# Seven-product down projection for 6 of 22 K pairs, its weight sums in the room of the transposed input, and operand tiles at one 2 KB remainder

## The chip, the cores and the metric

The kernel runs on one core of one Trainium2 chip. The metric is the device time of one execution in microseconds (us); of several executions the median is taken. The engines of the core are TensorE (PE; its loads of the stationary operand are PEld), VectorE (DVE), ScalarE (ACT), GpSimd (POOL) and SyncE (SP), whose queue issues nearly all transfers.

## What is computed

Two layers of a residual trunk over 256 tokens of width 2048. All data are float32.

```python
def swiglu(h, w_gate, w_up, w_down):
    return (jax.nn.silu(h @ w_gate) * (h @ w_up)) @ w_down

for l in range(DEPTH):                                   # 2 layers
    h = rms_norm(x, pre_mix_norm[l])
    m = hybrid_mixer(h, l, w_in[l], w_o[l], ...)          # stick-breaking and differential attention
    x = x + rms_norm(m, post_mix_norm[l])
    h = rms_norm(x, pre_ffn_norm[l])
    f = swiglu(h, w_gate[l], w_up[l], w_down[l])          # 2048 -> 5632 -> 2048
    x = x + rms_norm(f, post_ffn_norm[l])
```

The change concerns `@ w_down`: a product of 256 tokens x 5632 with 5632 x 2048, once in each layer.

## The kernel before

**Weights.** Every weight matrix is streamed once, in pieces of 256 rows (a K pair: two K blocks of 128) by 512 columns, 512 KB each. A piece lands in one of four `raw` buffers. A float32 piece is split in two: ACT rounds it to `hi` (L171), DVE forms the rest `lo = raw - hi` (L173). Both are of the type float32r. The stationary operands are split in the same way (`jh` and `jl` for the down projection, L852 and L854), and one float32 block product is three matmuls on PE, hi with hi, hi with lo, lo with hi, each of a 128x128 stationary and a 128x512 moving operand. `feed` prepares pieces four ahead of the one in use (`LOOKAHEAD`), six `hi` and six `lo` buffers hold them.

**Gate and up.** Eleven chunks `c` of 512 columns; in each, eight K pairs `kp`. For a K pair there are two token tiles, two K blocks and two matrices, hence eight block products, 24 matmuls (`eight`). For K pairs 2, 4 and 6 (in chunk 0: 4 and 6) a form with seven products is used (`seven`, 21 matmuls). It needs four sums of weights, formed on DVE (`mixed_weights`: `T`, L145) and split into `Th` (ACT, L154) and `Tl` (DVE, L156); four sums of token blocks (`token_sums`: `f` L738, `s` L741 to L744), split into `sh` (ACT, L746) and `sl` (DVE, L748); and four more PSUM banks, whose contents are combined on DVE at the end of a chunk (L811 to L815). `T`, `Th` and `Tl` (8, 12 and 12 KB of each partition) lie in the pool `gu`, which lives only through gate and up. In chunk 0 the two K pairs 0 and 1, then the `token_sums` of K pairs 2, 4 and 6 together, stand ahead of the other K pairs.

**Down.** Two halves, each of two column chunks of 512 (`cc`), over 22 K pairs (`nkp`). For each K pair `down` issues 24 matmuls (L872, L873, L875) into four PSUM banks. `prep` makes `jh` and `jl` up to two K pairs ahead. In the second half the last three K pairs (`TAIL`) are worked off one bank after the other (L894 to L896), so that a bank's result can be finished (`evac_chunk`: square with sum on ACT, L343; times the gain on DVE, L347) while PE works on the next. `rescale` then forms the norm and adds to `x`; in layer 0 the new `x` is transposed for the next layer (L274, L277, L282), in layer 1 it is stored (L363).

**Transposed input.** `xT` is 16 tiles of 2 KB of each partition, in the pool `wpool`, which lives through the whole kernel. It holds the input of the mixer, then that of gate and up; during down its room is reserved for the next layer's input, which is written at the end of down.

**Order.** The instructions of an engine run in the order in which the built program has them. A scheduler sets that order from the order in the code and its own estimates; `high_priority` and `manual_schedule` pin some of it. `tick` counts steps of the main matmul loop, and side work (attention, the transposes `flip` of each activated chunk) is started so many ticks later.

Of the kernel before, what the change touches and what calls it, by code (L numbers as in the profile page):

```python
# [37 lines left out]
FIRST_ORDER = (0, 1, 3, 2, 4, 5, 6, 7)  # L38

WARM = 13  # L40

# [6 lines left out]
def kernel(  # L48
# [152 lines left out]
    idle = const.tile([P, CW], BF16, name="idle")  # L201
# [10 lines left out]
    lams = const.tile([P, 4, L * 64], F32, name="lams")  # L212
    negones = const.tile([P, P], F32, name="negones")
# [6 lines left out]
    def late_constants():  # L220
# [16 lines left out]
        lprod = const.tile([P, 2, L * 64], F32, name="lprod")  # L237
        lsum = const.tile([P, 2, L], F32, name="lsum")
# [13 lines left out]

    eps = const.tile([P, 1], F32, name="eps")
# [38 lines left out]
    def x_tiles(nm):  # L292
        return [wpool.tile([P, 2, S], F32R, tag="xT", bufs=KT, name=f"{nm}_{k}") for k in range(KT)]
# [47 lines left out]
    def evac_chunk(pool, acc, mg, ssm, gpost, c, t, nm, mpool=None):  # L341
        junk = pool.tile([P, CW], F32, tag="t2", name=f"jm_{nm}_{t}_{c}")
        nc.scalar.activation(junk, acc, AF.Square, accum_out=ssm[t][:, c : c + 1])  # L343
        if c % 2 == 0:
            mg[t, c // 2] = (mpool or pool).tile([P, 2, CW], F32, tag="qk", bufs=4, name=f"mg_{nm}_{t}_{c}")
# [249 lines left out]
    def settle(pool, rs, evac):  # L595

        for t, h in ((0, 0), (0, 1), (1, 0), (1, 1)):
            load_x(t, h)
            yield 1
        late_constants()  # L600
        rs += [inv_rms(t, pool, "in0") for t in range(NT)]
        yield 2
        scales(rs)
        evac()
# [73 lines left out]

    xT = None
    for l in range(L):  # L680
# [52 lines left out]
        def token_sums(kp):  # L733

            f = pool.tile([P, 2, S], F32, tag="t2", name=f"f{l}_{kp}")
            for kk in range(2):
                st = xT[2 * kp + kk]
                nc.vector.tensor_tensor(out=f[:, kk, :], in0=st[:, 0, :].bitcast(F32), in1=st[:, 1, :].bitcast(F32), op=ALU.add)  # L738
            a11, a21, a12, a22 = f[:, 0, 0:P], f[:, 0, P:S], f[:, 1, 0:P], f[:, 1, P:S]
            s = pool.tile([P, 4, P], F32, tag="t2", name=f"s{l}_{kp}")  # L740
            nc.vector.tensor_tensor(out=s[:, 0, :], in0=a21, in1=a22, op=ALU.subtract)  # L741
            nc.vector.tensor_tensor(out=s[:, 1, :], in0=s[:, 0, :], in1=a11, op=ALU.subtract)
            nc.vector.tensor_tensor(out=s[:, 2, :], in0=a11, in1=a21, op=ALU.subtract)
            nc.vector.tensor_tensor(out=s[:, 3, :], in0=s[:, 1, :], in1=a12, op=ALU.add)  # L744
            sh = gu.tile([P, 4, P], F32R, tag="sh", bufs=len(SEVEN), name=f"sh{l}_{kp}")
            nc.scalar.activation(sh, s, AF.Copy)  # L746
            sl = gu.tile([P, 4, P], F32R, tag="sl", bufs=len(SEVEN), name=f"sl{l}_{kp}")
            nc.vector.tensor_tensor(out=sl, in0=s, in1=sh.bitcast(F32), op=ALU.subtract)  # L748
            forms[kp] = (sh, sl)

        def product(a, stat, moving, first, last):
            sh, sl = stat
            hi, lo = moving
            nc.tensor.matmul(a, sh, hi, start=first, stop=False)  # L754
            nc.tensor.matmul(a, sh, lo, start=False, stop=False)  # L755
            nc.tensor.matmul(a, sl, hi, start=False, stop=last)  # L756
# [11 lines left out]
        def seven(banks, extra, c, kp, first, last):  # L768
            hi, lo = weights(plan[l]["gate"][c, kp], LOOKAHEAD)
            m = weights(plan[l]["up"][c, kp], LOOKAHEAD)  # L770
            e, o = xT[2 * kp], xT[2 * kp + 1]
            sh, sl = forms[kp]
            s1, s2, s3, s4 = ((sh[:, j, :], sl[:, j, :]) for j in range(4))
            p1, p6, p7, q5 = extra
            todo = (
                (p1, (e[:, 0, 0:P], e[:, 1, 0:P]), (hi[:, 0, :], lo[:, 0, :]), first, last),
                (banks[0], (o[:, 0, 0:P], o[:, 1, 0:P]), (hi[:, 1, :], lo[:, 1, :]), False, False),
                (q5, s1, m["t1"], first, last),
                (p7, s3, m["t3"], first, last),
                (p6, s2, m["t2"], first, last),  # L780
                (banks[1], s4, m["b22"], False, False),
                (banks[2], (o[:, 0, P:S], o[:, 1, P:S]), m["t4"], False, False),
            )
            for n, job in enumerate(todo):
                if n % 2 == 0:
                    tick()
                product(*job)

        for c in range(FF // CW):
# [3 lines left out]
            if c == 0:  # L793
                for t in range(NT):
                    for kp in order[:2]:
                        eight(banks, c, kp, (t,), kp == order[0], False)
                for kp in SEVEN:
                    token_sums(kp)
                order = order[2:]
            extra = None  # L800
            for kp in order:
                if kp not in mine:
                    eight(banks, c, kp, range(NT), kp == 0, kp == order[-1])
                    continue
                if kp == mine[0]:
                    extra = four_banks(1 - c % 2, [f"{q}_{l}_{c}" for q in ("p1", "p6", "p7", "q5")])
                seven(banks, extra, c, kp, kp == mine[0], kp == mine[-1])
                if kp == mine[-1]:
                    p1, p6, p7, q5 = extra
                    w = [pool.tile([P, CW], F32, tag="t2", name=f"w{j}_{l}_{c}") for j in range(4)]  # L810
                    nc.scalar.copy(w[0], p1)  # L811
                    nc.vector.tensor_tensor(out=w[1], in0=p6, in1=w[0], op=ALU.add)
                    nc.vector.tensor_tensor(out=w[2], in0=p7, in1=w[1], op=ALU.add)
                    nc.vector.tensor_tensor(out=w[1], in0=q5, in1=w[1], op=ALU.subtract)
                    nc.vector.tensor_tensor(out=w[3], in0=q5, in1=w[2], op=ALU.subtract)  # L815
# [18 lines left out]
        gu.release()  # L834
        dn = tc.alloc_tile_pool(name=f"dn{l}", bufs=4, reuse_waits="tile")
# [6 lines left out]
        xT = x_tiles(f"xI{l}") if l + 1 < L else None  # L842

        for half in range(2):
            split = {}

            def prep(kp):
# [7 lines left out]
                split[kp] = (jh, jl)  # L855

            cc = (2 * half, 2 * half + 1)
            got = four_banks(1 - half, [f"dn{l}_{c}_{t}" for c in cc for t in range(NT)])
            accs = {(c, t): got[2 * (c % 2) + t] for c in cc for t in range(NT)}

            def down(kp, toks):
# [4 lines left out]
                for kk in range(2):  # L866
                    tick()
# [8 lines left out]

            tail = TAIL if half == 1 else 0
            for kp in range(nkp - tail):
                down(kp, range(NT))
            for t in range(NT):  # L880
                if not tail:
                    for c in cc:
                        evac_chunk(pool, accs[c, t], mg, ssm, gpost, c, t, f"d{l}", dn)
                    continue
                for c in cc:
# [11 lines left out]
                    with tc.high_priority(offset=URGENT):  # L897
                        evac_chunk(pool, accs[c, t], mg, ssm, gpost, c, t, f"d{l}", dn)
                with tc.high_priority(offset=URGENT):
                    rescale(mg, ssm, t, f"d{l}", store if xT is None else lambda t, c: transposed(t, (l + 1) * KT, xT, cols=(c,)))  # L900
        if l + 1 < L:
            rs = [inv_rms(t, pool, f"in{l + 1}") for t in range(NT)]
        dn.release()
# [50 lines left out]
```

## Time and profile before

| | |
|---|---|
| median of 3 runs | 2244.42 us (2244.08 to 2244.92) |
| the profiled execution | 2242.9 us, its span 2241.2 us |
| granted TensorE clock over the span | 0.997 |
| PE busy | 2223.1 us, 99% |
| DVE busy | 1623.8 us, 72% |
| ACT busy | 1221.8 us, 55% |
| moved by DMA | 423.72 MB, mean 189 GB/s |

A group row names line, engine, operation, result<-operands, their shapes and the count; behind the bar stand busy time and the mean of one in ns, then the idle time ahead of them and what ended it. A windows row gives for a stretch of time its length, then for each engine its busy time and (x) how many instructions ran, the granted clock as a share of full speed, the DMA share and GB/s. A timeline row gives the start, the time, engine, line, operation and operands; in brackets the idle time before it and who ended it. Matmuls overlap: a matmul's shown time is from its start to the modelled end of its results, so the distance from start to start tells the rate. DVE's instructions overlap by a little as well.

### The profile page before, as it was taken

To read this page: it belongs to the slowest core of one execution; us is meant where nothing else is said; L and a number is where in the kernel's file an instruction comes from. 1 tells how busy PE (TensorE), PEld (TensorE's weight loads), DVE (VectorE), ACT (ScalarE), POOL (GpSimd) and SP (SyncE) were. 2 spreads that over 40 slices of the span, in tenths; PEclk is the share of its full clock that TensorE was granted. 3 is DMA by queue.
4 is the path that set the end of the run, shared out by engine and by line. 5 is a ranking of instruction groups with operands and counts; after the bars stand their busy time and mean duration, and the time that the engine had idled before them with its cause. 6 is when DMAs were issued, how large, how long until landed. Compare 5 with 4: busy or idle time off the path is not lost.

```text
span 2241.2 us, 27963 instructions
## 1 busy us (share of the span) xinstructions
PE 2223.1 (99%) x10189; PEld 1829.8 (82%) x10189; DVE 1623.8 (72%) x2209; ACT 1221.8 (55%) x1819; POOL 37.0 (2%) x76
## 2 busy tenths in 40 slices
PE   9999999999999999999999999999999999999998
PEld 7788888788888888888887888887888888888887
DVE  6666555899899898565576665559998998975555
ACT  6555554665555556444565455546654555554443
POOL 1100000000000000000010000000000000000000
PEclk9999999999999999999999999999999999999999
DMA  8655555466556556555565555554666556565553
GB/s 295 191 165 163 160 188 185 134 205 213 192 188 215 198 188 224 189 189 197 178 195 163 173 157 168 186 181 147 210 204 205 189 197 207 191 215 189 194 198 134
DMA packets 217996, 423.72 MB, mean 189 GB/s; under 512 B 13569, under 2 KB 14081, under 8 KB 217345
## 3 DMA queue, kind: packets, MB, share of 16 engines
q1 hardware_dynamic: 217712, 421.91, 56.6%
q8 instruction: 80, 1.31, 0.2%
q14 instruction: 60, 0.48, 0.1%
q10 hardware_dynamic: 144, 0.02, 0.0%
HBM read 419.77 MB, written 2.10 MB: 188 GB/s over the span
## 4 chain that ended last, share of the span: by engine, by line
PE 95%; ACT 2%; DVE 1%; DMA 1%; issue 0%; SPq 0%; DVEq 0%; ACTq 0%
PE c L755 10%; PE c L756 10%; PE c L754 10%; PE in L336 8%; PE in L338 8%; PE in L337 8%; PE dn L872 7%; PE dn L873 7%; PE dn L875 7%; PE o L338 2%; PE o L336 2%; PE o L337 2%; PE p L754 2%; PE p L755 2%; PE p L756 2%; PE actT_ps L829 1%
## 5 line engine op out<-in xcount | busy, mean ns | idle before, releaser
L173 DVE TENSOR_TENSOR lo<-raw,hi 128x1024 fp32r<-128x1024 f32 x719 | 872.3, 1227 | 328.2 <-ACT hi L171 322.5
L171 ACT ACTIVATE hi<-raw 128x1024 fp32r<-128x1024 f32 x719 | 748.7, 1056 | 473.2 <-PE c L756 167.2
L754 PE MATMUL c<-hi,xF 128*128 128x512 f32 x960 | 377.1, 393 | 0.3
L756 PE MATMUL c<-hi,xF 128*128 128x512 f32 x960 | 374.4, 391 | 0.0
L755 PE MATMUL c<-lo,xF 128*128 128x512 f32 x960 | 373.9, 390 | 0.0
L872 PE MATMUL dn<-hi,jh 128*128 128x512 f32 x656 | 255.6, 390 | 0.0
L873 PE MATMUL dn<-lo,jh 128*128 128x512 f32 x656 | 255.2, 389 | 0.0
L756 PEld LDWEIGHTS c<-hi,xF 128*128 128x128 f32 x960 | 180.3, 188 | 37.6
L754 PEld LDWEIGHTS c<-hi,xF 128*128 128x128 f32 x960 | 180.6, 188 | 37.0 <-ACT xF L277 0.7
L755 PEld LDWEIGHTS c<-lo,xF 128*128 128x128 f32 x960 | 180.5, 188 | 36.7
L875 PE MATMUL dn<-hi,jl 128*128 128x512 f32 x656 | 202.0, 389 | 0.0
L154 ACT ACTIVATE Th<-T 128x1024 fp32r<-128x1024 f32 x128 | 135.2, 1057 | 114.0 <-DVE T L145 92.5
L854 DVE TENSOR_TENSOR jl<-act,jh 128x512 fp32r<-128x512 f32 x88 | 60.7, 692 | 161.1 <-ACT jh L852 161.1
L852 ACT ACTIVATE jh<-act 128x512 fp32r<-128x512 f32 x88 | 54.9, 631 | 219.3 <-PE dn L873 213.5
L156 DVE TENSOR_TENSOR Tl<-T,Th 128x1024 fp32r<-128x1024 f32 x128 | 156.3, 1221 | 2.5 <-ACT Th L154 1.2
L336 PE MATMUL in<-hi,xT 128*128 128x512 f32 x384 | 153.7, 401 | 0.7 <-ACT hi L171 0.7
L336 PE MATMUL in<-hi,xI 128*128 128x512 f32 x384 | 153.9, 401 | 0.0
L337 PE MATMUL in<-lo,xT 128*128 128x512 f32 x384 | 150.0, 391 | 1.0 <-DVE lo L173 1.0
L337 PE MATMUL in<-lo,xI 128*128 128x512 f32 x384 | 150.1, 391 | 0.3 <-DVE lo L173 0.3
L338 PE MATMUL in<-hi,xI 128*128 128x512 f32 x384 | 150.2, 391 | 0.0
L338 PE MATMUL in<-hi,xT 128*128 128x512 f32 x384 | 150.1, 391 | 0.0
L875 PEld LDWEIGHTS dn<-hi,jl 128*128 128x128 f32 x656 | 123.1, 188 | 25.7
(249 smaller groups left out, 3217.1 us busy)
## 6 DMA issues: line engine op xcount, KB each, us to landing
raw<-in_w_in_dram SPq DMA_DIRECT2D x191, 512.0 KB, 3.8
raw<-in_w_gate_dram SPq DMA_DIRECT2D x176, 512.0 KB, 3.6
raw<-in_w_up_dram SPq DMA_DIRECT2D x176, 512.0 KB, 4.4
raw<-in_w_down_dram SPq DMA_DIRECT2D x176, 512.0 KB, 4.3
raw<-in_w_o_dram SPq DMA_DIRECT2D x64, 512.0 KB, 4.2
xr<-in_x_columns_dram SPq DMA_DIRECT2D x8, 256.0 KB, 7.1
x<-in_x_dram SPq DMA_DIRECT2D x4, 512.0 KB, 7.8
gpost_mix<-in_post_mix_norm_dram SPq DMA_DIRECT2D x2, 1024.0 KB, 7.4
```

What stands on the lines that cost most here:

```text
L156: nc.vector.tensor_tensor(out=tl, in0=sums[j], in1=th.bitcast(F32), op=ALU.subtract)
L171: nc.scalar.activation(hi, raw, AF.Copy)
L173: nc.vector.tensor_tensor(out=lo, in0=raw, in1=hi.bitcast(F32), op=ALU.subtract)
L336: nc.tensor.matmul(a, sh, hi[:, kk, :], start=first and kk == 0, stop=False)
L337: nc.tensor.matmul(a, sh, lo[:, kk, :], start=False, stop=False)
L338: nc.tensor.matmul(a, sl, hi[:, kk, :], start=False, stop=last and kk == 1)
L754: nc.tensor.matmul(a, sh, hi, start=first, stop=False)
L755: nc.tensor.matmul(a, sh, lo, start=False, stop=False)
L756: nc.tensor.matmul(a, sl, hi, start=False, stop=last)
L872: nc.tensor.matmul(accs[c, t], sh, hi[:, kk, :], start=first, stop=False)
L873: nc.tensor.matmul(accs[c, t], sh, lo[:, kk, :], start=False, stop=False)
L875: nc.tensor.matmul(accs[c, t], sl, hi[:, kk, :], start=False, stop=last)
```

## The change

```diff
+FORM_AT = {1: 4, 3: 6, 5: 2}
+DOWN_SEVEN = (2, 5, 8, 11, 14, 17)
+LEVEL = 232
...
                 for c in (2 * half, 2 * half + 1):
                     lay["down"][c, kp] = queue_pair(w_down[l], kp, c)
+                if kp in DOWN_SEVEN:
+                    sevens.add(lay["down"][2 * half + 1, kp])
...
+    const.tile([P, LEVEL], F32, name="level")
...
-        return [wpool.tile([P, 2, S], F32R, tag="xT", bufs=KT, name=f"{nm}_{k}") for k in range(KT)]
+        return [x_pool[0].tile([P, 2, S], F32R, tag="xT", bufs=KT, name=f"{nm}_{k}") for k in range(KT)]
...
+    def evac_sum(pool, acc, mg, ssm, gpost, c, t, nm):
+        m = mg[t, c // 2][:, c % 2, :]
+        nc.vector.tensor_tensor(out=m, in0=acc, in1=m, op=ALU.add)
+        junk = pool.tile([P, CW], F32, tag="t2", name=f"jm_{nm}_{t}_{c}")
+        nc.scalar.activation(junk, m, AF.Square, accum_out=ssm[t][:, c : c + 1])
+        nc.vector.tensor_tensor(out=m, in0=m, in1=gpost[:, c * CW : (c + 1) * CW], op=ALU.mult)
...
+    def seven_products(banks, extra, sums, a11, a12, a22, hi, lo, m, first, last):
+        s1, s2, s3, s4 = sums
+        p1, p6, p7, q5 = extra
+        todo = (
+            (p1, a11, (hi[:, 0, :], lo[:, 0, :]), first, last),
+            (banks[0], a12, (hi[:, 1, :], lo[:, 1, :]), False, False),
+            (q5, s1, m["t1"], first, last),
+            (p7, s3, m["t3"], first, last),
+            (p6, s2, m["t2"], first, last),
+            (banks[1], s4, m["b22"], False, False),
+            (banks[2], a22, m["t4"], False, False),
+        )
...
-                for kp in SEVEN:
-                    token_sums(kp)
                 order = order[2:]
             extra = None
-            for kp in order:
+            for n, kp in enumerate(order):
+                if c == 0 and n in FORM_AT:
+                    pair_sums(FORM_AT[n])
...
         gu.release()
+        mix_pool[0] = new_x_pool(f"sums{l}")
...
-        xT = x_tiles(f"xI{l}") if l + 1 < L else None
...
                 split[kp] = (jh, jl)
+                if kp in DOWN_SEVEN:
+                    a11, a12, a21, a22 = src[:, 0, 0:P], src[:, 1, 0:P], src[:, 0, P:S], src[:, 1, P:S]
+                    forms[kp] = token_sums(pool, dn, 2, a11, a12, a21, a22, f"{l}_{half}_{kp}")
...
                 for kk in range(2):
+                    tick()
                     tick()
...
+            def down_seven(kp):
+                for n in range(3):
+                    prep(kp + n)
...
+                seven_products(got, extra, forms[kp], a11, a12, a22, hi, lo, m, kp == DOWN_SEVEN[0], kp == DOWN_SEVEN[-1])
...
             for kp in range(nkp - tail):
-                down(kp, range(NT))
+                if kp not in DOWN_SEVEN:
+                    down(kp, range(NT))
+                    continue
+                if kp == DOWN_SEVEN[0]:
+                    extra = four_banks(half, [f"{q}_d{l}_{half}" for q in ("p1", "p6", "p7", "q5")])
+                down_seven(kp)
+                if kp == DOWN_SEVEN[-1]:
+                    for t in range(NT):
+                        mg[t, half] = dn.tile([P, 2, CW], F32, tag="qk", bufs=4, name=f"mg_d{l}_{t}_{half}")
+                    shared_part(extra, [mg[t, half][:, j, :] for t in range(NT) for j in range(2)])
+            if half == 1:
+                xT = None
+                if l + 1 < L:
+                    new_x_pool(f"x{l + 1}")
+                    xT = x_tiles(f"xI{l}")
```

In words:

- **Down.** K pairs 2, 5, 8, 11, 14 and 17 of each half take the form with seven products. The two column chunks of a half stand where gate and up stood. `seven_products`, `token_sums` and `shared_part` (the former L811 to L815) are the old code of gate and up, now functions that both stages call. `token_sums` takes the activation directly, in `prep`, up to two K pairs ahead. The four extra banks of half 0 are those that half 1 accumulates in, and the other way round. After K pair 17 `shared_part` combines the extra banks into the four tiles `mg`, and `evac_sum` later adds each accumulating bank to its `mg` on DVE, squares that on ACT and multiplies by the gain on DVE. `down` ticks four times a K pair, as gate and up do, and no longer twice.
- **Room.** `xT` moves from `wpool` to a pool of its own at the upper end of memory. While down runs, that pool is released and the down stage's `T`, `Th` and `Tl` (32 KB) lie in its place (`sums0`, `sums1`); ahead of the tail of the second half it becomes the next layer's `xT`. Five tiles that only the first microseconds need move into a pool `setup`, released early.
- **Remainder.** A tile `level` of 928 bytes that nothing uses shifts the pools behind it. As built, the operand tiles of all split matmuls (moving `hi`, `lo`, `Th`, `Tl`; stationary `xT`, `mix`, `jh`, `jl`, `sh`, `sl`) start at 1632 modulo 2048 before and at 2016 modulo 2048 after.
- **Chunk 0.** The token sums of gate and up are formed one K pair at a time between the products of chunk 0: those of K pair 4 ahead of K pair 2's products, of 6 ahead of 5's, of 2 ahead of 7's.

More of the change, by code (lines that the diff above doesn't have):

```diff
@@ L738, in token_sums @@
                 nc.vector.tensor_tensor(out=f[:, kk, :], in0=st[:, 0, :].bitcast(F32), in1=st[:, 1, :].bitcast(F32), op=ALU.add)
[L739 to L756, printed above, removed]
+            forms[kp] = token_sums(pool, gu, len(SEVEN), f[:, 0, 0:P], f[:, 1, 0:P], f[:, 0, P:S], f[:, 1, P:S], f"{l}_{kp}")
         def eight(banks, c, kp, toks, first, last):
@@ L771, in seven @@
             e, o = xT[2 * kp], xT[2 * kp + 1]
[L772 to L787, printed above, removed]
+            a11, a12, a22 = (e[:, 0, 0:P], e[:, 1, 0:P]), (o[:, 0, 0:P], o[:, 1, 0:P]), (o[:, 0, P:S], o[:, 1, P:S])
+            seven_products(banks, extra, forms[kp], a11, a12, a22, hi, lo, m, first, last)
         for c in range(FF // CW):
@@ L808 @@
                 if kp == mine[-1]:
-                    p1, p6, p7, q5 = extra
                     w = [pool.tile([P, CW], F32, tag="t2", name=f"w{j}_{l}_{c}") for j in range(4)]
[L811 to L815, printed above, removed]
+                    shared_part(extra, w)
             at = pool.tile([P, 4, S], F32, tag="act", bufs=FF // CW, name=f"act{l}_{c}")
@@ L841 @@
         nkp = FF // P // 2
-        xT = x_tiles(f"xI{l}") if l + 1 < L else None
         for half in range(2):
-            split = {}
+            split, forms = {}, {}
             def prep(kp):
@@ L882 @@
                     for c in cc:
[L883 removed]
+                        evac_sum(pool, accs[c, t], mg, ssm, gpost, c, t, f"d{l}")
                     continue
```

65 lines of the change are left out of this document (54 added, 11 removed).

## Prediction

> **What bounds the kernel now.** I read the page first: busy times, then the chain that ended last, then the groups.
>
> ```profile
> PE 2223.1 (99%) x10189; PEld 1829.8 (82%) x10189; DVE 1623.8 (72%) x2209; ACT 1221.8 (55%) x1819; POOL 37.0 (2%) x76
> ...
> PE 95%; ACT 2%; DVE 1%; DMA 1%; issue 0%; SPq 0%; DVEq 0%; ACTq 0%
> ...
> L872 PE MATMUL dn<-hi,jh 128*128 128x512 f32 x656 | 255.6, 390 | 0.0
> ```
>
> PE is busy nearly throughout and makes 95% of the chain. The time is therefore the number of matmuls times their rate, plus the few places where PE waits. The 390 ns of a group are no rate, since matmuls overlap. The rate comes from counting, with the windows view of the down stage alone:
>
> ```profile
> 893.00:1100.00 207.00, 207.00 (x914) 171.37 (x914) 2.57 (x4) 2.53 (x8) 1.00 0.55 193
> 2007.00:2214.00 207.00, 207.00 (x913) 171.41 (x914) 2.57 (x4) 2.53 (x8) 1.00 0.55 193
> ```
>
> 914 matmuls in 207 us. A window also counts the one or two that reach into it, so the rate is 207/912.5 = 0.227 us a matmul, in both layers, at the full clock.
>
> Where PE waits, the waits view and the windows of the first chunk of gate and up tell:
>
> ```profile
> PE p L755 <- DVE lo L173: 3.6, 2, 1.8
> PE q L754 <- ACT Th L154: 2.1, 2, 1.1
> ...
> 427.00:438.00 11.00, 7.91 (x21) 4.96 (x20) 10.67 (x17) 4.22 (x6) 0.00 (x0) 0.71 0.30 99
> ...
> 1542.50:1553.50 11.00, 8.03 (x27) 5.14 (x26) 10.99 (x17) 4.27 (x5) 0.00 (x0) 0.84 0.32 108
> ```
>
> Both waits occur twice, once a layer, in the first K pair that is worked with seven products. In the 11 us around them 21 and 27 matmuls ran, where 11/0.227 = 48.5 fit: 27.5 x 0.227 = 6.2 us are lost in layer 0, 4.9 us in layer 1. The waits themselves are 3.6 + 2.1 = 5.7 us; most of the other 5.4 us is the clock, 0.71 and 0.84 of full. DVE is busy all through: it is what is late.
>
> **The matmuls that go.** A K pair with seven products has 21 matmuls for 24. Six pairs, two halves, two layers: 24 x 3 = 72 matmuls, x 0.227 = 16.3 us. The Trainium skill ("TensorE: Matmul & The Clock Gate", section "Back-to-back issue gap") gives about 131 ns for a sustained matmul of 512 columns, by which 72 would be 9.4 us. The two rows above contradict it, and the measurement decides.
>
> **What is added in the down stage, and where it hides.** The work goes to DVE first. Its price is taken from start to start, in the same operations in a steady stretch of gate and up and in chunk 0:
>
> ```profile
> 460.49 0.69 DVE L145 TENSOR_TENSOR T<-T,raw 128x512 f32<-128x512 f32 x1
> 461.09 0.68 DVE L150 TENSOR_TENSOR lo<-raw,hi 128x512 fp32r<-128x512 f32 x1
> ...
> 463.60 1.23 DVE L156 TENSOR_TENSOR Tl<-T,Th 128x1024 fp32r<-128x1024 f32 x1 [1.23 <-ACT Th L154]
> 464.74 1.22 DVE L173 TENSOR_TENSOR lo<-raw,hi 128x1024 fp32r<-128x1024 f32 x1
> ...
> 424.53 0.28 DVE L741 TENSOR_TENSOR s<-f 128x128 f32<-128x128 f32 x1
> 424.73 0.28 DVE L743 TENSOR_TENSOR s<-f 128x128 f32<-128x128 f32 x1
> ```
>
> So 1.14 us for 1024 columns, 0.60 for 512, 0.20 for 128. Take three K pairs of down, one of them with seven products. PE has 24 + 24 + 21 = 69 matmuls, 15.7 us. DVE has five whole pieces (5.7), four sums and a half piece (3.0), two `Tl` (2.3), three `jl` (1.8), four `s` (0.8), one `sl` (0.6): 14.2 us, 90% of PE's time. Before, it was 6 x 1.14 + 1.8 = 8.6 us. Is 90% too much for an engine that must keep order? Gate and up answer, with the same buffers and the same four pieces ahead: a chunk has 13 whole pieces (14.8), three sevens at 5.3 (15.9) and ten operations of some 0.6 for the result (6.1), 36.8 us, against 183 matmuls and 8 transposes, which by the row below take 380 x 191/1712 = 42.4 us: 87%; and between its pairs 2 and 6 it is denser, 23.7 (three sevens with their whole piece and two plain pairs) against 25.2 us. There PE does not wait:
>
> ```profile
> 470.00:850.00 380.00, 380.00 (x1712) 314.60 (x1711) 338.95 (x399) 212.12 (x245) 0.00 (x0) 1.00 0.60 201
> ```
>
> DVE is busy 89% there, PE all the time. I cost the sevens of down at nothing beyond their matmuls. The cover is DVE's remaining 1.5 us in three pairs, and the two pairs (10.9 us) by which pieces are prepared ahead. If it were gone, `lo` or `Tl` would be late as in chunk 0: 1.8 us at each of 24 places is the other end. I stand at the near end, since the nearest rows are 20 steady chunks without a wait.
>
> The first seven of each half needs a look, as DVE also finishes there what came before. Entering half 0 it has the last chunk's result: counted from the start of down, in the built order and at the prices above, four operations for it and two `jl` end at 3.3 us; four `s`, `lo`, two sums, `sl`, two sums and the half `lo` at 8.8; `Tl`, `jl` and the second `Tl` at 11.7. PE reaches K pair 2 after 48 matmuls and 8 transposes, at 11.8, and its fifth product, the first to need that `Tl`, four products (2.7 us) later, at 14.5. Cover 2.8 us. Half 1 opens with eight operations of `evac_sum` (4.8 us) and no result of gate and up, which is less. `shared_part` (2.4 us) falls to K pairs 18 to 21, where DVE needs 2.9 of 5.4 us.
>
> ACT splits two whole pieces of sums and two halves (a half piece, `sh`) at a seven, where it split one piece:
>
> ```profile
> L154 ACT ACTIVATE Th<-T 128x1024 fp32r<-128x1024 f32 x128 | 135.2, 1057 | 114.0 <-DVE T L145 92.5
> ...
> 875.50:1119.20 243.70, 243.70 (x1084) 201.59 (x1083) 144.28 (x158) 119.56 (x155) 0.00 (x0) 1.00 0.56 194
> ```
>
> With a half at 0.5 to 0.6, 2.2 us more, 26 us for a layer's twelve; it was busy 120 of 244 us of down. `T` in the room of `xT` waits for the last read of the tile it lies on, in the last chunk, whose matmuls stand ahead of down on PE: nothing. The extra banks are free by then too: in half 0 the last chunk's result and its two transposed copies on ACT, done about 10.6 us in; PE comes to the first bank that waits for a copy at 13.8. No transfer is added or moved.
>
> **Chunk 0, the moved sums.** Before, 18 forming operations stand on DVE ahead of the first piece that PE waits for:
>
> ```profile
> 422.18 0.42 DVE L738 TENSOR_TENSOR f<-xF 128x256 f32<-128x256 f32 x1
> ...
> 429.14 1.22 DVE L173 TENSOR_TENSOR lo<-raw,hi 128x1024 fp32r<-128x1024 f32 x1
> ...
> 425.71 1.06 ACT L171 ACTIVATE hi<-raw 128x1024 fp32r<-128x1024 f32 x1 [0.87 <-DMA raw<-in_w_up_dram]
> ...
> 426.99 0.39 PE L754 MATMUL p<-hi,xF 128*128 128x512 f32 x1
> ```
>
> In the built order that `lo` is now first, at 422.2, then the weight sums (to 426.6). `Th` queues on ACT behind the `hi` of 425.71, to 427.7 and 428.7; the second `Tl` ends at 430.4, the next two `lo` at 432.3 and 433.6 (with pieces of `s` between), `sh` at 434.4, `sl` at 435.5. PE arrives at 426.99 as before. After six matmuls, 428.35, it takes the product with the second `Th`: wait 0.4. Its `Tl` three matmuls later: wait 1.0. Four more, then `lo`: wait 0.95. Six more, and the other `lo`, `sh` and `sl` come in time, because the built order has put the products with `sh` some 23 matmuls later. Left are 2.35 us a layer, gained 6.2 - 2.35 and 4.9 - 2.35, together 6.4 us. The ends: nothing gained, or all 11.1 us.
>
> The clock is the uncertain part of it:
>
> ```profile
> 433.93 0.63 PE L755 MATMUL c<-lo,sh 128*128 128x512 f32 x1
> 434.36 0.63 PE L756 MATMUL c<-hi,sl 128*128 128x512 f32 x1
> ```
>
> After the waits matmuls came 0.43 us apart, not 0.227: the clock fell after waits of 1.8 and 1.1 us. Three waits of up to 1 us may or may not bring it down; I take that they do not, and a fall is a rival. The Trainium skill ("TensorE: Matmul & The Clock Gate", Part 1) has the clock halve after an idle window of some 3.4 us. By that rule it would stay up, and the sum would be as below; but in these rows it fell after waits that were each shorter than that, so the rule alone does not exclude a fall.
>
> **The end.** A bank is now added to its `mg` ahead of ACT's square:
>
> ```profile
> 2232.62 0.39 PE L896 MATMUL dn<-hi,jl 128*128 128x512 f32 x1
> ...
> 2233.05 0.60 ACT L343 ACTIVATE jm_d<-dn 128x512 f32<-128x512 f32 x1 [3.39 <-PE dn L896]
> ```
>
> One more DVE operation stands in this chain: 0.7 us at the end of layer 1. The multiplication by the gain stays beside the square. At the end of layer 0 the same step stands ahead of the transposes; I add 0.7 there (between 0, if the first products of the next layer cover it, and 1.5, if the add also queues behind a `lo`).
>
> **Remainder and room.** All operand tiles share one remainder before and after. What unequal ones may cost, one place hints at: the attention's `negtri` matmul, with operands at other remainders than the rest.
>
> ```profile
> L875 PE MATMUL dn<-hi,jl x656: 387/389/397, 879.4 to 2216.3; 128*128 128x512 f32 x164
> ...
> L454 PE MATMUL za_sb<-al_sb,negtri x8: 393/393/393, 233.9 to 1445.3; 128*128 128x512 f32 x8
> ```
>
> That is 4 ns more than a matmul of down. With equal remainders I take 0; the other end is 4 ns for each of the 10189 matmuls, 41 us.
>
> **Sum.** 2242.9 (profiled execution) - 16.3 - 6.4 + 0.7 + 0.7 = 2221.6. The median of the runs, 2244.42, lies 1.5 above that execution, so I forecast 2223 (own range 2220 to 2226).
>
> **Rivals.** *Chunk 0 keeps its loss* (the waits move but stay, or the clock falls again): 6.4 us less gained, 2229. For it: DVE stays full there. *Chunk 0's loss goes wholly*: 4.7 us more, 2218; against it: three waits remain on paper. *Some sevens late*, as the first of each half, or a few more: four to eight times 1.8, 2230 to 2237; for it: only 2.8 us of cover, and a queue at 90%. *Every seven late*: DVE cannot hold the pace of down, `lo` or `Tl` comes 1.8 us late each time: 24 x 1.8 = 43, so 2266, slower. It decides from DVE work of more than 15.7 us in three pairs, and eats the gain from 0.9 us a seven; for it 14.2 us is a sum of best cases, against it the steady chunks. *The remainder does not do what it says*: at 2016 or across pools each matmul costs 4 ns: 2223 + 41 = 2264. Against it: the tiles are equal as built.
>
> **Chances.** Forecast 0.50; chunk 0 keeps its loss 0.14; its loss goes 0.11; some late 0.15; every seven late 0.06; remainder 0.02; a gain just eaten up 0.02. A measurement of this kernel can tell 0.2%, 4.5 us, from no change: faster 0.90, same 0.02, slower 0.08. Range 2215 to 2238.
>
> **What would show it.** Right: 72 PE instructions fewer; 0.227 us a matmul in the down windows, with no PE wait on `lo`, `Th` or `Tl` there; DVE about 90% busy between K pairs 2 and 17; in the 11 us around 427 some 38 matmuls at a clock near 1; PE's last matmul to the end 0.7 us longer. Wrong: a `lo` or `Tl` that ends PE waits once per three pairs, a clock below 1 in down, or matmuls at another distance than 0.227 us.

## The result, and the profile after

| | before | after |
|---|---|---|
| median | 2244.45 us (2244.08 to 2244.92, 4 runs) | 2226.47 us (2225.40 to 2228.93, 4 runs) |
| ratio, 95% interval | | 0.9921 [0.9904, 0.9939] |
| profiled execution, its span | 2242.9, 2241.2 us | 2225.4, 2223.6 us |

The changed kernel is faster by 18.0 us. That is inside the range (2215 to 2238), 3.5 us above the forecast of 2223, and just outside the likeliest case's own range of 2220 to 2226. The two profiled executions lie 17.5 us apart. To see where these come from I cut the time into stages, each from the start of its first matmul to the start of the next stage's first, as the trace's PE rows give them ("mixer in, 1" begins with the first matmul of the input projection and holds most of the 32 transposes between the layers, 24 before and 28 after; "end" is from the last matmul's start to the last instruction's end):

| us | gate and up, 0 | down, 0 | mixer in, 1 | gate and up, 1 | down, 1 | end |
|---|---|---|---|---|---|---|
| before | 476.02 | 241.39 | 302.06 | 474.70 | 240.11 | 8.55 |
| after | 474.74 | 233.14 | 303.70 | 472.65 | 231.88 | 9.34 |
| difference | -1.28 | -8.25 | +1.64 | -2.05 | -8.23 | +0.79 |
| predicted | -3.85 | -8.16 | +0.7 | -2.55 | -8.16 | +0.7 |

The stages left out changed by 0.8 us at most. At the boundary of the layers two small things cancel in "down, 0": four transposes (about 0.5 us) left it for "mixer in, 1", and a new wait of 0.39 us stands at its end. Down of layer 1, which has neither, became shorter by nearly the same, 8.23 us, so the 1.64 us can be read as what the boundary lost. First the page's busy times:

```profile
PE 2205.6 (99%) x10117; PEld 1814.4 (82%) x10117; DVE 1765.9 (79%) x2505; ACT 1276.3 (57%) x1895; POOL 37.4 (2%) x76
```

72 matmuls fewer, and 296 DVE instructions more. The windows of the down stage, layer 0 and layer 1:

```profile
893.00:1100.00 207.00, 207.00 (x915) 171.41 (x914) 187.40 (x258) 126.86 (x161) 0.00 (x0) 1.00 0.62 206
1985.00:2192.00 207.00, 207.00 (x919) 171.49 (x918) 191.82 (x267) 131.98 (x167) 0.00 (x0) 1.00 0.60 199
```

Again 207 us hold 913.5 matmuls or a few more: the rate is unchanged, 0.227 us at most, PE is busy all the time, and DVE went to 91% and 93%. The two halves of the forecast for down, that the matmuls go at their full rate and that DVE keeps up, hold to 0.1 us a layer. What PE does wait for is elsewhere, by the waits view of the kernel after:

```profile
PE c L707 <- DVE Tl L161: 1.6, 2, 0.8
...
PE c L707 <- DVE lo L178: 1.0, 2, 0.7
PE c L706 <- ACT w L743: 0.8, 1, 0.8
PE xT_ps L290 <- DVE x L378: 0.8, 1, 0.8
...
PE c L706 <- ACT Th L159: 0.5, 1, 0.5
PE in L352 <- ACT xI L293: 0.4, 1, 0.4
```

No row of it is of down (`dn`, `p_d`, `q_d`). The rows with `c` lie in chunk 0 and at the start of chunk 1. The two windows of 11 us of that place, the same distance into the stage as those of before:

```profile
427.00:438.00 11.00, 8.98 (x31) 6.26 (x30) 10.06 (x16) 5.83 (x7) 0.00 (x0) 0.84 0.63 188
1534.00:1545.00 11.00, 9.77 (x40) 7.01 (x40) 10.38 (x17) 5.88 (x7) 0.00 (x0) 1.00 0.62 192
```

31 and 40 matmuls, where 21 and 27 had run and "some 38" were forecast: the second is as forecast, in the first the clock fell to 0.84. From the matmul starts of chunk 0 (a wait is the distance of two starts less 0.227 us; the waits view shows less, since it counts from a matmul's modelled end), the waits at the first K pair in seven products are 0.68, 0.99 and 0.85 us in layer 0 (forecast 0.4, 1.0 and 0.95) and 0.98, 0.22 and 0.63 in layer 1. But then 0.62 us (layer 0) and 0.97 us (layer 1) follow, 11 to 22 us after the last of these: in the last pair of chunk 0, right behind the second K pair in seven products, and in chunk 1. The forecast had ended its walk before them. In layer 0 eight matmuls that start 0.43 us apart come on top, which costs 1.6 us; and after each wait the next start comes 0.34 us later in place of 0.227, together some 0.9 us in the two layers.

At the layer boundary DVE's queue tells the rest. Its timeline at the end of layer 0, first of the kernel before, then of the one after:

```profile
1111.57 0.16 DVE L351 TENSOR_REDUCE tot_d<-ssm_d 128x1 f32<-128x4 f32 x1 [3.39 <-ACT jm_d L343]
...
1113.10 0.75 DVE L355 SCALAR_TENSOR_TENSOR x<-mg_d,tot_d,x 128x512 f32<-128x512 f32 x1
```

```profile
1102.71 0.16 DVE L374 TENSOR_REDUCE tot_d<-ssm_d 128x1 f32<-128x4 f32 x1 [0.79 <-ACT jm_d L369]
...
1103.73 1.22 DVE L178 TENSOR_TENSOR lo<-raw,hi 128x1024 fp32r<-128x1024 f32 x1 [0.20 <-ACT hi L176]
...
1105.14 1.23 DVE L178 TENSOR_TENSOR lo<-raw,hi 128x1024 fp32r<-128x1024 f32 x1
...
1107.01 1.22 DVE L178 TENSOR_TENSOR lo<-raw,hi 128x1024 fp32r<-128x1024 f32 x1
1108.14 0.74 DVE L378 SCALAR_TENSOR_TENSOR x<-mg_d,tot_d,x 128x512 f32<-128x512 f32 x1
```

From the sum of squares to the first new piece of `x` it was 1.5 us before and is 5.4 us after: three `lo` now stand between the short steps of the norm. The transposes of the first token tile start 0.4 us ahead of the last matmul of down, where they had started 5.7 us ahead.

The end of layer 1 is as forecast; the timeline shows the added step:

```profile
2214.31 0.39 PE L955 MATMUL dn<-hi,jl 128*128 128x512 f32 x1
2214.74 0.69 DVE L367 TENSOR_TENSOR mg_d<-dn,mg_d 128x512 f32<-128x512 f32 x1 [0.33 <-PE dn L955]
2215.46 0.63 ACT L369 ACTIVATE jm_d<-mg_d 128x512 f32<-128x512 f32 x1 [1.78 <-DVE mg_d L367]
```

From the last matmul's start to the square it was 0.43 us and is 1.15.

### The profile page after: what moved, and what is told of

The parts are those of the page before. It is cut to its first block, busy times and chain, and to the rows that moved or that the text cites. A ratio compares the mean times of both kernels' runs of the same rounds, so it can differ in the third digit from the quotient of the medians.

```text
span 2223.6 us, 28156 instructions
## 1 busy us (share of the span) xinstructions
PE 2205.6 (99%) x10117; PEld 1814.4 (82%) x10117; DVE 1765.9 (79%) x2505; ACT 1276.3 (57%) x1895; POOL 37.4 (2%) x76
## 4 chain that ended last, share of the span: by engine, by line
PE 94%; ACT 2%; DVE 1%; DMA 1%; issue 0%; SPq 0%; DVEq 0%; ACTq 0%
PE c L707 10%; PE c L706 10%; PE c L708 10%; PE in L352 8%; PE in L354 8%; PE in L353 8%; PE dn L911 5%; PE dn L909 5%; PE dn L908 5%; PE o L354 2%; PE o L352 2%; PE o L353 2%; PE p L706 2%; PE p L707 2%; PE p L708 2%; ACT hi L176 1%
## 5 line engine op out<-in xcount | busy, mean ns | idle before, releaser
L178 DVE TENSOR_TENSOR lo<-raw,hi 128x1024 fp32r<-128x1024 f32 x695 | 843.9, 1224 | 309.6 <-ACT hi L176 304.4
L176 ACT ACTIVATE hi<-raw 128x1024 fp32r<-128x1024 f32 x695 | 726.9, 1056 | 497.8 <-PE in L354 164.9
L159 ACT ACTIVATE Th<-T 128x1024 fp32r<-128x1024 f32 x176 | 185.7, 1056 | 141.7 <-DVE T L150 133.8
L161 DVE TENSOR_TENSOR Tl<-T,Th 128x1024 fp32r<-128x1024 f32 x176 | 214.2, 1217 | 4.4 <-ACT Th L159 3.8
L908 PE MATMUL dn<-hi,jh 128*128 128x512 f32 x464 | 180.7, 389 | 0.0
L909 PE MATMUL dn<-lo,jh 128*128 128x512 f32 x464 | 180.5, 389 | 0.0
L911 PE MATMUL dn<-hi,jl 128*128 128x512 f32 x464 | 142.8, 389 | 0.0
L150 DVE TENSOR_TENSOR T<-T,raw 128x512 f32<-128x512 f32 x176 | 120.5, 684 | 1.2
L911 PEld LDWEIGHTS dn<-hi,jl 128*128 128x128 f32 x464 | 87.1, 188 | 18.1
L908 PEld LDWEIGHTS dn<-hi,jh 128*128 128x128 f32 x464 | 87.1, 188 | 18.1
```

The source lines that it names most:

```text
L161: nc.vector.tensor_tensor(out=tl, in0=sums[j], in1=th.bitcast(F32), op=ALU.subtract)
L176: nc.scalar.activation(hi, raw, AF.Copy)
L178: nc.vector.tensor_tensor(out=lo, in0=raw, in1=hi.bitcast(F32), op=ALU.subtract)
L908: nc.tensor.matmul(accs[c, t], sh, hi[:, kk, :], start=first, stop=False)
L909: nc.tensor.matmul(accs[c, t], sh, lo[:, kk, :], start=False, stop=False)
L911: nc.tensor.matmul(accs[c, t], sl, hi[:, kk, :], start=False, stop=last)
```

## The experiments

Ten kernels ran, each timed beside the kernel before on the same chip. Ratios are to that kernel, with the 95% interval. The median of the kernel before lay between 2243.6 and 2244.5 us on each occasion, so differences to the changed kernel, which was timed on another one, are good to about 1 us.

**The moved sums alone.** The kernel before, with only the sums of token blocks of chunk 0 formed one at a time between K pairs.

```diff
+FORM_AT = {1: 4, 3: 6, 5: 2}
...
-                for kp in SEVEN:
-                    token_sums(kp)
...
+                if c == 0 and n in FORM_AT:
+                    token_sums(FORM_AT[n])
```

> The kernel before with one part of the change alone: in chunk 0 of gate and up the token sums are formed one K pair at a time. Theory (the sums alone make the gain that the changed kernel shows in gate and up, 1.3 us in layer 0 and 2.1 in layer 1): 2244.4 - 3.4 = 2241, down as before at 241.4 and 240.1 us. Rival (that gain comes with the other pools or the longer DVE queue of down): 2244, gate and up at 476.0 and 474.7 us as before.

Measured: 2240.30 us (2239.21 to 2242.84, 10 runs), ratio 0.9987 [0.9977, 0.9996], 3.3 us less than before. The windows of chunk 0:

```profile
427.00:438.00 11.00, 9.23 (x39) 6.63 (x38) 9.79 (x17) 5.89 (x8) 0.00 (x0) 1.00 0.58 184
1540.50:1551.50 11.00, 9.78 (x40) 6.96 (x39) 10.25 (x17) 5.95 (x7) 0.00 (x0) 1.00 0.61 190
```

39 and 40 matmuls as forecast, at the full clock. Here too the later waits (1.1 and 1.0 us a layer) took part of the gain away. So about 3.3 us of the change's 18 come from the moved sums; the forecast had 6.4.

**Sevens in half 0 alone.** The changed kernel with no K pair in seven products in half 1, whose banks are then finished as before the change.

```diff
...
-                if kp not in DOWN_SEVEN:
+                if kp not in DOWN_SEVEN or half == 1:
...
-                        evac_sum(pool, accs[c, t], mg, ssm, gpost, c, t, f"d{l}")
+                        evac_chunk(pool, accs[c, t], mg, ssm, gpost, c, t, f"d{l}")
```

> The changed kernel with seven products in half 0 alone; half 1 is as before, with the square on ACT straight from the bank and no add. Theory (a seven saves 3 x 0.227 us and no more, and what the layer's end lost comes of the added step): down about 4.1 us longer in each layer, the stretch from the last product of down to the end 0.8 us shorter, and the first stage of layer 1 back from 303.7 to about 302 us: 2226.5 + 8.2 - 0.8 - 1.7 = 2232. Rival (the layer's end lost its time to the shared room or to another order): the first stage of layer 1 stays at 303.7, 2234.

Measured: 2232.53 us (2231.95 to 2234.82), ratio 0.9951 [0.9935, 0.9968]. Down is 4.09 and 4.07 us longer than with both halves, 18 matmuls by 0.227 us, and the end is 8.56 us again. The boundary gave back 0.9 us of 1.64. The rest is a wait of this kernel that the one before hardly had (it waited 0.3 us there):

```profile
PE xT_ps L290 <- DVE x L378: 1.0, 1, 1.0
```

It does not come from the order: on ACT and DVE the same operations stand there as before. ACT's timeline shows what is later, first in the kernel before, then in this one:

```profile
1118.74 1.06 ACT L171 ACTIVATE hi<-raw 128x1024 fp32r<-128x1024 f32 x1 [0.53 <-DMA raw<-in_w_in_dram]
```

```profile
1114.55 1.06 ACT L176 ACTIVATE hi<-raw 128x1024 fp32r<-128x1024 f32 x1 [1.39 <-DMA raw<-in_w_in_dram]
```

One piece of the next layer's weights was issued at the same distance from the boundary, but took 4.51 us in this execution and 3.64 before; ACT waited 0.86 us longer for it, and what follows on ACT and DVE, the new `x` included, is later by about as much. Why the transfer took longer is not shown.

**Nine sevens a half.** Every second K pair from 2 to 18, to see where DVE's pace decides.

```diff
-DOWN_SEVEN = (2, 5, 8, 11, 14, 17)
+DOWN_SEVEN = (2, 4, 6, 8, 10, 12, 14, 16, 18)
```

> The changed kernel with nine pairs of 22 in a half with seven products, every second one from 2 to 18. 36 matmuls fewer, 8.2 us. Theory (DVE's work of two pairs, 11.3 us from start to start, is what then sets the pace, against 10.2 us of PE): from K pair 2 to 18 DVE needs 99 us a half and PE 86, less up to 11 us of work ahead, so 2 to 12 us of waits on lo and Tl in each half, and 2226 to 2266, not faster. Rival (DVE keeps up, the price from start to start is too high): 2226.5 - 8.2 = 2218.

Measured: 2267.45 us (2265.41 to 2271.50), ratio 1.0110 [1.0095, 1.0125]: slower, and slightly above the upper end of what was expected. Down takes 260.0 and 251.7 us, where 18 matmuls fewer a layer would by themselves have made it 4.1 us shorter than the changed kernel's 233.1 and 231.9. A window of down, then the waits view:

```profile
890.00:960.00 70.00, 67.25 (x287) 52.63 (x286) 67.65 (x102) 41.81 (x54) 0.00 (x0) 1.00 0.55 179
```

```profile
PE p_d L706 <- ACT hi L176: 7.5, 16, 1.5
PE xT_ps L290 <- DVE x L378: 6.8, 1, 6.8
PE q_d L707 <- DVE Tl L161: 6.0, 6, 1.5
PE p_d L706 <- ACT Th L159: 5.7, 17, 1.5
```

DVE is busy 97% there, and PE runs 287 matmuls where 308 fit (70/0.227). Most of these waits name ACT, but ACT itself waits for pieces, and the queue that fetches them waits for DVE to free their buffers. The waits of ACT and of the queue's SyncE, in down of layer 0 (880 to 1110 us):

```profile
ACT hi L176 <- DMA raw<-in_w_down_dram: 75.2, 38, 3.4
```

```profile
SPq L139 <- DVE lo L178: 89.7, 43, 4.6
SPq L139 <- DVE T L150: 89.2, 16, 5.9
```

In the changed kernel ACT waits 11.5 us for pieces there, and in the kernel before not at all. This is the forecast's rival "every seven late", at two pairs for a seven instead of three. By the prices of the forecast a plain pair costs DVE 2 x 1.14 + 0.60 = 2.9 us and one in seven products 14.2 - 2 x 2.9 = 8.4, together 11.3, against 45 x 0.227 = 10.2 us of PE: 111%. The same prices gave 90% for three pairs, and there PE did not wait.

**No spacer.** The changed kernel without `level`. The pools on the left then lie 1088 bytes past a multiple of 2 KB, those on the right 2016 past one; 5856 of the matmuls then have a moving and a stationary tile that start at different remainders, 2304 of the input projections, 3264 of gate and up and 288 of down, and none of the output projection (the expectation's 5880 is 24 too many).

```diff
-    const.tile([P, LEVEL], F32, name="level")
```

> The changed kernel without the unused tile `level`: the pools of the lower end, with hi, lo, mix, jh, jl, sh, sl and gate and up's T, start at 1088 modulo 2048, those of the upper end, with the transposed input and down's T, stay at 2016. 5880 matmuls then have a moving and a stationary operand of unequal remainder (all of the input projection, most of gate and up, few of down, none of the output projection). Theory (unequal remainders cost the 4 ns by which the attention's matmul stood out): 24 us, so 2250, all of it in the input projection and in gate and up. Rival (the remainder is of no account): 2226.

Measured: 2260.81 us (2260.41 to 2261.22), ratio 1.0078 [1.0063, 1.0093], 34.3 us above the changed kernel. Windows of gate and up and of the output projection, of the changed kernel:

```profile
480.00:850.00 370.00, 370.00 (x1669) 306.48 (x1668) 331.87 (x392) 208.08 (x240) 0.00 (x0) 1.00 0.62 201
...
330.00:390.00 60.00, 60.00 (x278) 49.98 (x277) 32.98 (x37) 29.75 (x50) 0.00 (x0) 1.00 0.59 185
```

and without the spacer:

```profile
480.00:850.00 370.00, 370.00 (x1625) 298.94 (x1624) 324.14 (x379) 202.37 (x231) 0.00 (x0) 1.00 0.62 199
...
330.00:390.00 60.00, 60.00 (x279) 50.00 (x278) 33.77 (x38) 30.12 (x49) 0.00 (x0) 1.00 0.57 178
```

PE is busy all the time in both, at the full clock, and does 44 matmuls fewer in 370 us of gate and up, while the projection with equal remainders runs as before. By stages, the input projections became 5.9 and 5.6 us longer, gate and up 10.3 and 10.9, down 1.2 each, and what follows from the output projection to gate and up not at all. 34.3 us over 5856 matmuls are 5.9 ns each.

**Thirty-two bytes.** The spacer 8 elements longer: left pools at 0, right pools at 2016, 32 bytes apart round the 2 KB.

```diff
-LEVEL = 232
+LEVEL = 240
```

> The changed kernel with the left pools at remainder 0 of 2 KB and the right ones at 2016, 32 bytes apart round the 2 KB, where the kernel without the spacer has them 928 bytes apart (and cost 34 us). If any difference costs the same, 2260. If the cost goes by the distance, 34 x 32/928 = 1 us: 2227 to 2228.

Measured: 2257.65 us (2256.87 to 2259.10), ratio 1.0061 [1.0047, 1.0074], 31.2 us above the changed kernel.

```profile
480.00:850.00 370.00, 370.00 (x1629) 299.42 (x1628) 325.99 (x381) 202.64 (x231) 0.00 (x0) 1.00 0.62 199
```

32 bytes cost nearly what 928 do. The cost by distance is refuted: these runs show a cost of being unequal, to within some 3 us. PE's timeline of this run has both kinds side by side, in the middle of gate and up; tiles `Th`, `Tl` and `hi` share their remainder with `sh` and `sl`, but not with `xF`:

```profile
600.63 0.39 PE L706 MATMUL q<-Th,sh 128*128 128x512 f32 x1
...
603.12 0.40 PE L708 MATMUL c<-hi,sl 128*128 128x512 f32 x1
603.36 0.39 PE L706 MATMUL c<-Th,xF 128*128 128x512 f32 x1
...
606.39 0.40 PE L707 MATMUL c<-lo,xF 128*128 128x512 f32 x1
```

Eleven steps between equal tiles take 2.49 us, 0.226 each; thirteen between unequal ones 3.03 us, 0.233 each. From 480 to 850 us the means are 0.227 and 0.233. (Without the spacer, `Th` and `Tl` with `sh` and `sl` also took 0.232 in gate and up, although their tiles start at equal remainders there too; that is not explained.)

What has to be equal is less than the remainder of 2 KB. `down` reads its stationary operand 0, 512, 1024 or 1536 bytes from the start of its tile and its moving one 0 or 2048 bytes; in the kernel before, where all tiles start at one remainder, each of these combinations runs at 0.226 to 0.227 us from start to start (medians of 42 K pairs). A difference that is a multiple of 512 bytes thus costs nothing. And 928 and 32 are both odd multiples of 32, so it is open whether a difference of 64, 128 or 256 bytes costs anything.

**One seven less in chunk 0.** The changed kernel with only K pair 6 in seven products in chunk 0.

```diff
-FIRST_SEVEN = (4, 6)
+FIRST_SEVEN = (6,)
-FORM_AT = {1: 4, 3: 6, 5: 2}
+FORM_AT = {2: 6, 4: 2, 5: 4}
```

> The changed kernel with one K pair less in seven products in chunk 0 of gate and up (only K pair 6), its sums formed later: 3 matmuls more a layer, 2 x 3 x 0.227 = 1.4 us. Theory: what chunk 0 still loses (4.9 us in layer 0 and 2.8 us in layer 1 of the profiled execution of the changed kernel) belongs to DVE's work for its first K pair with seven products, K pair 4, which has no steady stretch ahead of it in which DVE could get ahead. Then nearly all of the 7.7 us goes: 2226.5 + 1.4 - 7.7 = 2220. Rival: the loss moves on to the next such K pair, 6, as the second one of layer 1 (1.0 us, at K pair 6) hints: only some 2 us go, 2226 to 2228.

Measured: 2218.58 us (2217.81 to 2219.74), ratio 0.9886 [0.9873, 0.9900]: faster, 7.9 us less than the changed kernel, with six matmuls more. Windows of chunk 0:

```profile
427.00:438.00 11.00, 11.00 (x51) 9.09 (x50) 10.50 (x18) 6.27 (x8) 0.00 (x0) 1.00 0.66 225
1530.00:1541.00 11.00, 11.00 (x50) 9.11 (x49) 10.86 (x17) 6.26 (x8) 0.00 (x0) 1.00 0.67 227
```

PE does not wait at all here, and both layers' gate and up take 469.9 us. That makes a measure for what chunk 0 lost before: 476.02 - 469.89 + 0.68 (three matmuls) = 6.8 us in layer 0 and 5.5 in layer 1; after the change still 5.5 and 3.4, 8.9 together, where the expectation counted 7.7. The edit also forms the sums of a K pair one or two K pairs later, and what that does by itself was not measured.

**No seven in chunk 0.** The same with none.

```diff
-FIRST_SEVEN = (4, 6)
+FIRST_SEVEN = ()
-FORM_AT = {1: 4, 3: 6, 5: 2}
+FORM_AT = {3: 2, 4: 4, 5: 6}
...
```

The rest of the edit finishes chunk 0 without the combination of the extra banks.

> The changed kernel with no K pair in seven products in chunk 0: 6 matmuls more a layer, 2.7 us in all, four banks' combination less. If the sevens are the cause of chunk 0's loss, all of 7.7 us goes and the time is 2226.5 + 2.7 - 7.7 = 2221.5, with no PE wait in the 11 us where there were three, and a clock near 1. Rival: chunk 0 loses because the pieces of weights come late after the change of stage (transfers, or the 18 forming operations by themselves): then the waits stay and the time is 2229.

Measured: 2219.39 us (2218.89 to 2220.93), ratio 0.9891 [0.9877, 0.9904]. The two windows have no PE wait either. Gate and up take 470.57 and 470.58 us, 0.68 and 0.66 more than with one seven, the price of the three matmuls. K pair 6 in seven products hence costs nothing beyond its matmuls; it is K pair 4, with only four pairs ahead of it, that comes too early.

**One seven less, sums ahead.** K pair 6 alone in seven products, but all three sums formed ahead, as before the change.

```diff
-FIRST_SEVEN = (4, 6)
+FIRST_SEVEN = (6,)
-FORM_AT = {1: 4, 3: 6, 5: 2}
...
+                for kp in SEVEN:
+                    pair_sums(kp)
...
```

> One K pair less in seven products in chunk 0, but all three sums formed ahead, as before the change: 18 forming operations of DVE, some 4.7 us, in one stretch after K pair 1. Theory: what makes chunk 0 late is the first K pair with seven products itself, and the sums only add to it; with five plain pairs ahead of K pair 6 DVE makes up the 4.7 us, and the time is that with the sums moved, 2218.6 within 0.5. Rival: the sums by themselves make lo late for the plain pairs, as the wait of 1.8 us before the change: 2222 or more.

Measured: 2226.32 us (2225.82 to 2226.71), ratio 0.9919 [0.9906, 0.9933]. My theory falls: the sums by themselves cost 7.7 us, also with plain pairs behind them. DVE's timeline in chunk 0 of layer 0 shows how:

```profile
425.26 0.42 DVE L806 TENSOR_TENSOR f<-xF 128x256 f32<-128x256 f32 x1
426.79 1.29 DVE L719 TENSOR_TENSOR sl<-s,sh 128x512 fp32r<-128x512 f32 x2 [1.11 <-ACT sh L717]
...
428.61 1.22 DVE L177 TENSOR_TENSOR lo<-raw,hi 128x1024 fp32r<-128x1024 f32 x1
```

DVE works off the sums from 421.8, stands 1.1 us for ACT's `sh`, and comes to the plain pairs' `lo` at 428.6. PE's timeline:

```profile
429.88 0.50 PE L706 MATMUL c<-lo,xF 128*128 128x512 f32 x1 [2.25 <-DVE lo L177]
...
432.39 0.63 PE L706 MATMUL c<-lo,xF 128*128 128x512 f32 x1
...
434.79 0.39 PE L705 MATMUL c<-hi,xF 128*128 128x512 f32 x1
```

PE waits 2.25 us for that `lo`, and from 1.6 us after the wait on, its matmuls start 0.43 us apart, for some 3 us. So chunk 0 had two causes, each enough by itself: the sums in one stretch, and a first seven after four pairs.

**A seventh seven in half 0.** K pair 20 as well, in half 0 alone.

```diff
-DOWN_SEVEN = (2, 5, 8, 11, 14, 17)
+DOWN_SEVEN = ((2, 5, 8, 11, 14, 17, 20), (2, 5, 8, 11, 14, 17))
...
```

The rest of the edit reads `DOWN_SEVEN[half]` in place of `DOWN_SEVEN`.

> The changed kernel with a seventh such K pair, 20, in half 0 of down: 3 matmuls less a layer, 1.4 us, so 2225.1 if DVE holds the pace as it did with six. Rival: the combination of the extra banks (2.4 us of DVE) now falls after K pair 20, where the half's end and the first pieces of half 1 need DVE too; then lo or a bank of half 1 is late by 1 to 2 us a layer, and the time is 2226 to 2229.

Measured: 2226.85 us (2224.95 to 2227.35), ratio 0.9919 [0.9905, 0.9933], the time of the changed kernel. Down did become 0.66 and 0.69 us shorter, and nothing waits in it, so the rival's time was met without the rival's cause. The profiled execution, 2227.35 us, lost 1.4 us in gate and up of layer 1 (474.05 us for 472.65) and 1.9 in the mixer's input after the boundary (305.56 for 303.70), where the clock fell:

```profile
1115.00:1150.00 35.00, 33.15 (x150) 26.65 (x149) 26.51 (x63) 23.34 (x53) 5.34 (x8) 0.95 0.59 188
```

Two of the five executions took 2225.0 and 2225.1 us, which is the theory's time; the profiled one is the longest of the other three.

**Both edits.** One seven less in chunk 0 and one more in half 0 of down.

```diff
-FIRST_SEVEN = (4, 6)
+FIRST_SEVEN = (6,)
-FORM_AT = {1: 4, 3: 6, 5: 2}
-DOWN_SEVEN = (2, 5, 8, 11, 14, 17)
+FORM_AT = {2: 6, 4: 2, 5: 4}
+DOWN_SEVEN = ((2, 5, 8, 11, 14, 17, 20), (2, 5, 8, 11, 14, 17))
...
```

> Two edits together: one K pair less in seven products in chunk 0 (2218.6 by itself) and one more, K pair 20, in half 0 of down. The second made down 0.66 to 0.69 us shorter in each layer where it ran alone, and what it lost was a clock of 0.95 after the waits at the layer boundary. Theory: 2218.6 - 1.4 = 2217.2. Rival: the boundary's waits bring the clock down here too, and 1.9 us go again: 2219.

Measured: 2216.69 us (2216.45 to 2217.17), ratio 0.9877 [0.9863, 0.9890]: the fastest version, 27.7 us (1.2%) below the kernel before it, and its four runs lie within 0.7 us of each other, where the changed kernel's four spread over 3.5.

## Why the prediction came out as it did

*The matmuls that go* (-16.3): right. Down became 8.25 and 8.23 us shorter, together 16.5, and half the sevens are worth half of it. The rate that was counted in the trace, 0.227 us, held. The figure of the Trainium skill ("TensorE: Matmul & The Clock Gate", section "Back-to-back issue gap"), by which it would have been 9.4, did not apply to these matmuls.

*The new sevens cost nothing beyond their matmuls*: right, and so was the reason: 90% worked out, 91 and 93% seen, no PE wait in down; at every second pair, 111% on paper, they are late. (The denser stretch of gate and up, 23.7 us in the forecast, is 23.9 by its own prices; nothing hangs on it.) The rival "every seven late" and its turning point were the right ones to name, and were on the other side of it. The cover of 2.8 us at the first seven of a half held too: in layer 0 the second `Tl` ended 2.8 us ahead of its matmul.

*Chunk 0, the moved sums* (-6.4): the mechanism was right, the size was not: it gained 3.3 us in the profiled pair (1.28 and 2.05 us in the two stages) and 3.3 alone. By the measure of the experiment with one seven less, chunk 0 lost 12.3 us before and 8.9 after, where the forecast had 11.1 and 4.7. So the term that was mis-sized is what remains after the change. The three waits were within 0.3 us of those forecast in layer 0, but the walk along the built order ended at the first seven and called what followed in time; behind the second one and in the next chunk another 0.6 to 1.0 us are lost in each layer. The late restart after each wait, some 0.9 us in all, was not counted. The forecast took the clock to stay up; it fell in layer 0 of the profiled execution, at a price of 1.6 us, though no wait was longer than 1.0 us. What was lost before was taken from windows of 11 us, 6.2 and 4.9, where the whole stage lost 6.8 and 5.5; that slip alone would have made the gain larger.

On the clock, the rule of the Trainium skill ("TensorE: Matmul & The Clock Gate", Part 1), a fall after an idle window of some 3.4 us, would have kept it up. This trace does not agree: here it fell after waits of 0.68, 0.99 and 0.85 us within some 4.3 us, and in the experiment with the sums ahead after one wait of 2.25 us; in layer 1 it did not after waits of 0.98, 0.22 and 0.63 us. The lengths of the waits do not settle it either: with sevens in half 0 alone, layer 1 has waits of 1.01, 0.99 and 0.85 us before the same three matmuls and kept its clock (1.00 from 1537 to 1548 us). So what decides, and how much of one run's time hangs on this, stays open. The changed kernel's runs spread by 3.5 us and those of the versions without waits in chunk 0 by 0.7 to 2.0; but the version without the spacer, which has the waits, spread by 0.8.

*The end of layer 1* (+0.7): right, 0.79. *The end of layer 0* (+0.7): 1.64, beyond the upper bound of 1.5. The step that failed is the one that priced the added add alone. The operation itself costs 0.7; but the norm starts later in the built order, and three `lo` of the next layer now run between its serial steps. The bound had one such `lo` in it. Where half 1 was finished as before, with the old order, 0.9 us of the loss went, and the 0.7 left there goes with a transfer that took 0.87 us longer in that execution.

*The remainder at nothing*: right by both experiments. The other end, 4 ns for each matmul, was too small a price for too many matmuls: it is 5.9 ns for each of the 5856 that are unequal, 34 us. The 4 ns came from shown times, whose ends are modelled; the distances from start to start, 0.233 against 0.227 us, tell the price. Without the spacer the changed kernel would be slower than before.

Of the rivals, "chunk 0 keeps its loss" (2229) was the nearest to what happened: half of what was to go stayed. The two terms, 3.1 us less from chunk 0 and 0.9 us more at the boundary, are 4.0, against the 3.8 us by which the profiled execution (2225.4) missed the sum (2221.6).

## What to carry to other kernels

Count the side engine's work over the period in which the pattern repeats, against the time that the bounding engine takes for it: 90% held without a wait and 111% did not. Then look at the starts, where the side engine has no lead: four pairs ahead of the first costly step were too few, six were enough once the sums were spread out, and giving that step up there, at the price of six matmuls, gained 7.9 us. A step that is added ahead of a serial chain is not priced by its own length, but by what the engine's queue puts between the chain's steps once they start later: read that from the built order.

## What the runs showed of the hardware

A float32r matmul whose moving and stationary tiles start 928 or 32 bytes apart, modulo 2 KB, takes 5 to 7 ns longer: 34.3 us over 5856 matmuls at 928 bytes, 31.2 us at 32 bytes, and 0.233 against 0.226 us from start to start within one run. Differences of 512, 1024 and 1536 bytes cost nothing (0.226 to 0.227 us). The busy share of PE does not show it, only counting matmuls or their starts does.

The granted clock fell in one profiled execution after three waits of no more than 1 us each within some 4.3 us, and stayed up in others after three that were as long. The slow stretch, with matmuls 0.43 us apart, lasted some 3 us in the changed kernel and up to 5 in the kernel before (433.5 to 438.5 us), and began up to 1.6 us after PE had started again, so that a part of the price of a wait stands in the rows behind it.
